# One layer of a streaming encoder in fp32: the order of loads around the output projection, the turn and the down sweep

## The chip, the cores and the metric

One core of a Trainium2 chip runs the whole layer. The metric is the device time of one execution in microseconds: the kernel before takes 1625.86 us, the median of three runs (1624.2 to 1626.41). The engines are TensorE (PE), VectorE (DVE), ScalarE (ACT), GpSimd (POOL) and SyncE (SP); all loads and most stores are issued from SP's queue, in its order.

## The reference

The layer has attention in two head groups, an output projection with a residual and a layer norm, a gated convolutional feed-forward block with a residual and a second norm, and a gated addition of a per-layer embedding. It runs for 1024 prompt rows and for 32 rows of a second request (the samples), with shared weights. What the change touches lies behind the attention, in `mix @ w_o` and the feed-forward block:

```python
mix = jnp.concatenate([o_a.reshape(b, s, H_A * D_VA), o_b.reshape(b, s, W_B)], -1)
return mix @ lp['w_o'], (c_kv, k_r, dk, dv)
...
u = h @ lp['w_up']                                  # 1024 -> 2 x 2816
up = jnp.concatenate([conv_state, u], 1)
z = lp['conv_b'] + sum(up[:, j:j + s] * lp['conv_w'][j] for j in range(CONV_W))
g, v = z[..., :D_FF], z[..., D_FF:]
out = (jax.nn.gelu(g, approximate=False) * v) @ lp['w_down']
...
h = _ln(ALPHA * x + a, lp['ln1_g'], lp['ln1_b'])
h = _ln(ALPHA * h + f, lp['ln2_g'], lp['ln2_b'])
gate = jax.nn.sigmoid(h @ lp['w_ple_gate'] + lp['b_ple_gate'])
y = h + gate * (p_emb @ lp['w_ple_proj'])
```

All inputs and outputs are fp32.

## The kernel before

**Arithmetic.** PE multiplies in fp32r, a rounded form of fp32. Each operand x is split into a high half (an ACT cast, L85) and a low half (a subtraction, L82, on DVE or POOL), and a product is three matmuls: high by high, high by low, low by high (`three`, L144 to L146). The 32 sample rows ride with high and low halves side by side and need two (`sample_rows`, L152 and L153). A weight tile is loaded to a staging tile by SP (`load`, L112) and split by ACT and DVE (`wload`).

**Tiles.** `pair()` takes a tile from a pool HP of 22 (names h...), `slab()` one of 4 (s...), `stg()` one of 2 staging tiles (t...); PSUM has four tiles pm and two pd. A tile's next user waits until its last reader is done. The rows are nine tiles of 128: 8 is the samples, and 7 down to 0 the prompt; `order` is 8, 7, ..., 0. The rows `arow(t)` hold x first, then h, then the output; four HP tiles hold the prompt's.

**The order of the work.** The program text is not the order on the engines. The kernel is built with a scheduler that simulates a timeline and places each instruction by it; dependencies, pool tiles and a `gate` (loads that may not go ahead of a named instruction) bind it. Each engine then runs its list strictly in that order.

**The stages.** Behind the attention, the mixed heads of a tile are split (`mix_in`), multiplied with w_o in four blocks of 256 columns (`wo_block`, `proj_rows`) and added to ALPHA times x (`residual`, L1026). Blocks 0 and 1 run over all tiles, block by block; blocks 2 and 3 run tile by tile in `h_rows`, which ends with the norm (`unit`) and a store of the normalised row to DRAM (`hrow`), since HP is needed for other things. `h_turn` transposes a row tile on PE (L1102) and copies it from PSUM with the norm's scale and bias applied (eight ACT activations, L1104). `h_pair` and `h_sample` make the operands of the up-projection from it, which is a Strassen-Winograd scheme: seven products (L1217 to L1219) on half-sized blocks, for each of two column halves b.

The up-projection runs over 22 pairs m of 128-wide blocks of the feed-forward width (`UpPair`). For each pair the weights are loaded two ahead (`up_load`), combined and split one ahead (`UpWeights.part`); `finish` gives six steps (`todo`: three taps of the convolution, gelu, gating, store to DRAM tensor `zd`), which run between the products of the next pair.

The down sweep runs over four groups of 6, 6, 6 and 4 blocks. For each group it takes the weights (`wdown`: a 512 KB load and a split per block) and then, per row tile, loads and splits z (`z_in`, 384 KB) and adds two 512-wide products to the row (`down_rows`); in group 0 the row is loaded back and multiplied with ln1 ahead of that (L1365, L1366). The last group is in `y_norm`, tile by tile together with the second norm, the gate and the output.

## Time and profile before

| | |
|---|---|
| median of three runs | 1625.86 us |
| profiled execution, its own time | 1623.54 us |
| its span | 1621.7 us |
| PE busy | 1515.6 us (93%) |
| DVE busy | 950.9 us (59%) |
| ACT busy | 724.2 us (45%) |
| POOL busy | 337.5 us (21%) |
| chain that ended last | PE 83%, DVE 7%, ACT 5%, DMA 3% |

The span is from the first to the last instruction of the profiled execution; its own time has some two microseconds around that. Busy time is an average over the whole layer; the stages named above lie one behind the other, the first w_o block from about 590 us, the turn about 706 to 738, the up-projection to about 1183, the down sweep's first three groups from 1202 to 1422, its last group to the end.

A row of the timeline gives start and duration of an instruction, engine, line, operation, output and input, and in brackets the idle time of its engine before it with what ended it.

### The profile page before, as it was taken

The page shows a single profiled execution, that of the slowest core. Times are in us where ns is not written, and L with a number is a line of the kernel's source. Part 1 is how long each engine was busy: PE and PEld are TensorE (multiplying, and loading weights), DVE is VectorE, ACT ScalarE, POOL GpSimd, SP SyncE. Part 2 cuts the span into 40 slices and gives each one's busy share as a digit, 9 for nine tenths or more (in the row PEclk, how much of TensorE's full clock was granted, in tenths as well). Part 3 has the DMA queues.
Part 4 walks back from the last instruction along what each step waited for, and adds up shares of the span by engine and source line. Part 5 has one row for each costly group of instructions (what it writes and reads, how often), then busy time and mean ns, then how long its engine had stood idle before and what let it go on. Part 6 is the DMA issues. An engine that isn't in the chain of part 4 may idle for free.

```text
span 1621.7 us, 25780 instructions
## 1 busy us (share of the span) xinstructions
PE 1515.6 (93%) x10015; PEld 1377.2 (85%) x10015; DVE 950.9 (59%) x1914; ACT 724.2 (45%) x1787; POOL 337.5 (21%) x394
## 2 busy tenths in 40 slices
PE   7999998888989979989999999999949999979998
PEld 7999987777878869979999999999938787856887
DVE  4013328786767655487677777777777524256332
ACT  4222438777777752185455555555442202111111
POOL 0002225532554310011011111111100000157311
PEclk9999999989999999999999999999979999989999
DMA  7112251311110241123122222222165424130111
GB/s 220 30 48 83 79 166 39 69 41 21 36 36 15 69 173 31 53 92 105 40 80 79 80 80 80 80 80 79 67 199 176 134 54 133 65 96 20 42 43 42
DMA packets 126943, 127.92 MB, mean 79 GB/s; under 512 B 14750, under 2 KB 107558, under 8 KB 126566
## 3 DMA queue, kind: packets, MB, share of 16 engines
q1 hardware_dynamic: 126821, 126.28, 25.6%
q8 instruction: 79, 1.29, 0.3%
q14 instruction: 43, 0.34, 0.1%
HBM read 93.83 MB, written 26.07 MB: 74 GB/s over the span
## 4 chain that ended last, share of the span: by engine, by line
PE 83%; DVE 7%; ACT 5%; DMA 3%; issue 1%; SPq 0%; POOL 0%; DVEq 0%; ACTq 0%
PE pm L144 14%; PE pm L146 14%; PE pm L145 14%; PE pd L1217 5%; PE pd L1219 5%; PE pd L1218 5%; PE pm L1217 4%; PE pm L1219 4%; PE pm L1218 4%; PE pm L813 2%; DVE h L82 2%; ACT h L85 2%; PE pm L152 1%; PE pm L153 1%; PE pm L579 1%
## 5 line engine op out<-in xcount | busy, mean ns | idle before, releaser
L144 PE MATMUL pm<-h,h 128*128 128x256 f32 (+4 forms) x1140 | 378.9, 332 | 13.3 <-ACT h L85 8.8
L146 PE MATMUL pm<-h,h 128*128 128x256 f32 (+4 forms) x1140 | 374.9, 330 | 2.6 <-DVE h L82 2.6
L145 PE MATMUL pm<-h,h 128*128 128x256 f32 (+4 forms) x1140 | 375.2, 329 | 0.0
L144 PEld LDWEIGHTS pm<-h,h 128*128 128x128 f32 x1140 | 217.7, 191 | 32.7 <-ACT h L85 9.6
L146 PEld LDWEIGHTS pm<-h,h 128*128 128x128 f32 x1140 | 216.2, 190 | 19.3 <-DVE h L82 3.0
L145 PEld LDWEIGHTS pm<-h,h 128*128 128x128 f32 x1140 | 216.7, 190 | 16.5 <-issue 0.5
L85 ACT CAST h<-t 128x1024 fp32r<-128x1024 f32 (+6 forms) x97 | 88.2, 920 | 232.6 <-PE pm L146 121.7
L82 DVE TENSOR_TENSOR h<-t,h 128x1024 fp32r<-128x1024 f32 (+6 forms) x87 | 92.4, 1071 | 106.7 <-ACT h L85 106.4
L82 DVE TENSOR_TENSOR h<-pm,h 128x256 fp32r<-128x256 f32 (+7 forms) x221 | 101.5, 485 | 55.8 <-ACT h L85 53.9
L1230 DVE SCALAR_TENSOR_TENSOR h<-h,cp,h 128x1058 f32<-128x1058 f32 x88 | 115.7, 1316 | 29.8 <-ACT h L1238 29.1
L1217 PE MATMUL pm<-h,s 128*128 128x264 f32 x360 | 103.1, 288 | 10.1 <-ACT s L85 10.1
L85 ACT CAST h<-pm 128x256 fp32r<-128x256 f32 (+7 forms) x221 | 88.2, 425 | 53.7 <-PE pm L804 22.2
L1204 ACT COPY h<-pd 128x256 f32<-128x256 f32 (+1 forms) x258 | 56.2, 270 | 118.0 <-PE pd L1219 117.7
L1218 PE MATMUL pm<-h,s 128*128 128x264 f32 x360 | 102.3, 286 | 0.0
L1219 PE MATMUL pm<-h,s 128*128 128x264 f32 x360 | 101.0, 288 | 0.2 <-DVE s L82 0.2
L1217 PE MATMUL pd<-h,s 128*128 128x264 f32 x344 | 98.1, 285 | 0.0
L1219 PE MATMUL pd<-h,s 128*128 128x264 f32 x344 | 98.0, 285 | 0.0
L1218 PE MATMUL pd<-h,s 128*128 128x264 f32 x344 | 97.9, 285 | 0.0
L82 DVE TENSOR_TENSOR h<-h,h 128x512 fp32r<-128x512 f32 (+3 forms) x160 | 93.1, 617 | 3.5 <-ACT h L85 2.1
L178 POOL TENSOR_TENSOR sm<-sm,neghalf 128x1 f32<-128x1 f32 (+1 forms) x37 | 24.2, 653 | 275.6 <-DVE sm L177 275.6
L1347 DVE TENSOR_TENSOR h<-pm,h 128x512 f32<-128x512 f32 x48 | 33.1, 689 | 82.3 <-PE pm L146 82.2
L1217 PEld LDWEIGHTS pm<-h,s 128*128 128x128 f32 x360 | 68.6, 191 | 10.7 <-ACT s L85 10.5
(319 smaller groups left out, 3728.3 us busy)
## 6 DMA issues: line engine op xcount, KB each, us to landing
h<-in_w_up SPq DMA_DIRECT2D x44, 512.0 KB, 4.5
zd<-h SPq DMA_DIRECT2D x22, 529.0 KB, 4.3
t<-in_w_down SPq DMA_DIRECT2D x22, 512.0 KB, 3.5
t<-zd SPq DMA_DIRECT2D x24, 384.0 KB, 4.0
h<-in_x_p SPq DMA_DIRECT2D x15, 512.0 KB, 6.9
t<-in_w_in SPq DMA_DIRECT2D x14, 512.0 KB, 4.0
h<-h SPq DMA_DIRECT2D x8, 512.0 KB, 4.3
t<-in_w_o SPq DMA_DIRECT2D x8, 512.0 KB, 3.6
```

The source lines that it names most:

```text
L82: return eng.tensor_tensor(out, x, y, ALU.subtract)
L85: c = ACT.copy(hi, src)
L144: PE.matmul(ps, sh, mh, start=(i == 0), stop=False)
L145: PE.matmul(ps, sh, ml, start=False, stop=False)
L146: PE.matmul(ps, sl, mh, start=False, stop=(i == last))
L813: PE.matmul(po[:, c : c + 256], vt[k // 4][:, k % 4, h % 4], pts[k // 4][:, hl, k % 4], start=(k == 0 and hl == 0), stop=(k == kt - 1 and ...
L1204: ACT.copy(x, y)
L1217: PE.matmul(ps[:, :BW], w[:, 0, k], c[:, k, 0], start=first and k == 0, stop=False, skip_group_check=True)
L1218: PE.matmul(ps[:, :BW], w[:, 0, k], c[:, k, 1], start=False, stop=False, skip_group_check=True)
L1219: PE.matmul(ps[:, :BW], w[:, 1, k], c[:, k, 0], start=False, stop=k == 3, skip_group_check=True)
L1230: DVE.scalar_tensor_tensor(z[:, j], U[:, j, i : i + T], cp[:, i, m + j * NF : m + j * NF + 1], z[:, j], ALU.mult, ALU.add)
L1347: DVE.tensor_tensor(d, ps[:n], d, ALU.add)
```

## The change

The loads and splits around these stages are issued at other places in the program; a few are also shaped differently.

1. **w_o stage.** Instead of all nine x rows at once, three are loaded first and the rest two tiles ahead inside the first loop, and the mixed heads are split two tiles ahead (before: one). The second w_o block is issued at the second tile. The last two 256-column blocks become one of 512, and `h_rows` has one 512-wide projection instead of two. The first up weights are loaded and combined in the second block's loop; before, they were combined between row tiles and products. The small convolution and norm tables are loaded ahead of the x rows, as the loops now stand behind them in the text.
2. **The turn.** `h_turn` copies odd blocks with DVE and even ones with ACT. The pair (1,1) and the samples' half 1 are made ahead of the last row tile, and all seven products of half 0 stand before the pair (1,0).
3. **Down sweep.** The six weights of group 0 are loaded as three tiles of two blocks (1 MB) during the last two up pairs and split between the products of the last pair. z, and in group 0 the rows, are fetched two tiles ahead; the next group's weights are issued at the fifth tile of each group; z of the first two tiles of the last group is fetched at the end of group 2. The last pair's finish steps run one per tile in group 0 instead of all before it. The rows' HP tiles are taken one by one, when the row comes back.

```diff
@@ -1045,28 +1045,13 @@
         (eng or POOL).tensor_tensor(r, r, g[:n, :D], ALU.mult)
         (eng or POOL).tensor_tensor(r, r, b[:n, :D], ALU.add)
-    for t in order:
+    def x_back(t):
         load(arow(t)[: TOK[t][1]], a["x_p"][t * 128 : (t + 1) * 128, :] if t < 8 else a["x_s"])
-    wb.append(wo_block(256, 256))
-    mix_in(order[1])
-    for i in range(2):
-        wb.append(wo_block(256 * (i + 2), 256))
-        for m, t in enumerate(order):
-            if i == 0 and 1 < m + 1 < 9:
-                mix_in(order[m + 1])
-            ps, ps2 = proj_rows(t, wo_at(wb[i], 256), 256)
-            residual(t, 256 * i, 256, ps, ps2)
-    hrow = [DR.tile([128, 1024], F32, name=nm("hrow")) for _ in range(8)]
-    def h_rows(t):
-        for i in (2, 3):
-            ps, ps2 = proj_rows(t, wo_at(wb[i], 256), 256)
-            residual(t, 256 * i, 256, ps, ps2)
-        unit(arow(t)[: TOK[t][1]], TOK[t][1])
-        if t < 8:
-            SP.dma_start(hrow[t], arow(t))
+    for t in order[:3]:
+        x_back(t)
+    for t in order[1:3]:
+        mix_in(t)
@@ -1101,7 +1086,10 @@
         for j in range(8):
             PE.transpose(ps[:, j, :n], arow(t)[:n, j * 128 : (j + 1) * 128], ident[:n, :n])
         for j in range(8):
-            ACT.activation(d[:, j], ps[:, j, :n], AF.Identity, bias=lnT[:, 8 + j : 9 + j], scale=lnT[:, j : j + 1])
+            if j % 2:
+                DVE.tensor_scalar(d[:, j], ps[:, j, :n], lnT[:, j : j + 1], lnT[:, 8 + j : 9 + j], ALU.mult, ALU.add)
+            else:
+                ACT.activation(d[:, j], ps[:, j, :n], AF.Identity, bias=lnT[:, 8 + j : 9 + j], scale=lnT[:, j : j + 1])
     def h_pair(b, q):
@@ -1258,9 +1246,37 @@
     zd = [DR.tile([128, len(fs), T], F32, name=nm("zd")) for fs in GROUPS]
+    for i in range(2):
+        for m, t in enumerate(order):
+            if i == 0:
+                if m == 1:
+                    wb.append(wo_block(256, 256))
+                if 2 < m + 2 < 9:
+                    x_back(order[m + 2])
+                    if m:
+                        mix_in(order[m + 2])
+            elif m == 0:
+                wb.append(wo_block(512, 512))
+                wts = UpWeights(up_load(0))
+            if i == 1 and m < NP:
+                wts.part(m)
+            ps, ps2 = proj_rows(t, wo_at(wb[i], 256), 256)
+            residual(t, 256 * i, 256, ps, ps2)
+    hrow = [DR.tile([128, 1024], F32, name=nm("hrow")) for _ in range(8)]
+    def h_rows(t):
+        ps, ps2 = proj_rows(t, wo_at(wb[2], 512), 512)
+        residual(t, 512, 512, ps, ps2)
+        unit(arow(t)[: TOK[t][1]], TOK[t][1])
+        if t < 8:
+            SP.dma_start(hrow[t], arow(t))
     for t in order[:4]:
         h_rows(t)
-    hs = slab()
+    hs = small(512, tag="sam", bufs=1)
     V["hs"], V["hs2"] = hs[:, :256].rearrange("p (k c) -> p k c", k=8), hs[:, 256:512]
     h_turn(8, V["hs"])
     h_rows(4)
@@ -1268,41 +1284,49 @@
     h_sample(0)
     h_rows(3)
     h_pair(0, 0)
-    R = up_load(0)
     h_rows(2)
-    wts = UpWeights(R)
-    wts.part(0)
-    wts.part(1)
     h_rows(1)
-    for i in range(2, 5):
-        wts.part(i)
+    h_pair(1, 1)
+    h_sample(1)
     h_rows(0)
     u = UpPair(0)
     u.ps[0, 0] = pm()
-    for i in range(3):
-        u.product(wts.w[i], i, 0)
-    h_pair(1, 1)
-    for i in range(3, 5):
-        u.product(wts.w[i], i, 0)
-    h_sample(1)
-    for i in range(5, NP):
-        wts.part(i)
+    for i in range(NP):
         u.product(wts.w[i], i, 0)
     h_pair(1, 0)
-    R = up_load(1)
-    nxt = UpWeights(R)
+    nxt = UpWeights(up_load(1))
+    gate[0] = None
+    acc = {}
+    wrows, wfirst = {}, []
+    def wd_load(fi):
+        wrows[fi // 2] = pair((128, 2, 1024), F32)
+        load(wrows[fi // 2], w_dn[:, fi : fi + 2])
+    def wd_part(fi):
+        w = pair()
+        split(w[:, 0, :1024], w[:, 1, :1024], wrows[fi // 2][:, fi % 2])
+        wfirst.append(w)
     todo = []
-    gate[0] = None
     for m in range(NF):
         if m:
             u = UpPair(m)
         if m + 2 < NF:
             R = up_load(m + 2)
+        else:
+            wd_load(2 * (m + 2 - NF))
         for i in range(NP):
             for b in range(2) if m else (1,):
                 u.product(wts.w[i], i, b)
             if m + 1 < NF:
                 nxt.part(i)
+            elif i < 6:
+                if i == 2:
+                    wd_load(4)
+                wd_part(i)
             if todo:
                 todo.pop(0)()
         todo = u.finish()
@@ -1311,11 +1335,7 @@
             nxt = UpWeights(R)
         if m == NF - 2:
             gate[0] = UnitF[0]
-    for s in todo:
-        s()
-    acc = [pair((128, 2, 1024), F32) for _ in range(4)]
     def wdown(fs, eng=None):
         return [wload([(0, 1024, w_dn[:, fi])], 1024, eng) for fi in fs]
@@ -1353,22 +1373,44 @@
     ln1 = [slab() for _ in range(2)]
     for i, key in enumerate(("ln1_g", "ln1_b")):
         load(ln1[i][:, :D], a[key].to_broadcast([128, D]))
+    def row_back(t):
+        n = TOK[t][1]
+        if t < 8 and t // 2 not in acc:
+            acc[t // 2] = pair((128, 2, 1024), F32)
+        r = arow(t)[:n]
+        if t < 8:
+            load(r, hrow[t])
+        DVE.tensor_tensor(r, r, ln1[0][:n, :D], ALU.mult)
+        DVE.tensor_tensor(r, r, ln1[1][:n, :D], ALU.add)
     gate_last = UnitF[0]
+    ahead = {}
+    def z_ahead(g, t):
+        if g == 0:
+            row_back(t)
+        ahead[g, t] = z_in(g, t)
+    ws = wfirst
+    for t in order[:2]:
+        z_ahead(0, t)
     for g in range(3):
-        ws = wdown(GROUPS[g])
-        for t in order:
+        for m, t in enumerate(order):
+            for c in (0, 512):
+                down_rows(g, t, ws, ahead[g, t], c)
+            if m + 2 < 9:
+                z_ahead(g, order[m + 2])
+            else:
+                z_ahead(g + 1, order[m - 7])
             if g == 0:
-                n = TOK[t][1]
-                r = arow(t)[:n]
-                if t < 8:
-                    load(r, hrow[t])
-                DVE.tensor_tensor(r, r, ln1[0][:n, :D], ALU.mult)
-                DVE.tensor_tensor(r, r, ln1[1][:n, :D], ALU.add)
-            z = z_in(g, t)
-            for c in (0, 512):
-                down_rows(g, t, ws, z, c)
-        if g == 0:
-            gate[0] = gate_last
+                for st in todo[:1]:
+                    todo.pop(0)()
+            if m == 4:
+                nxt = wdown(GROUPS[g + 1])
+        ws = nxt
+        gate[0] = gate_last
     ps = pm()
@@ -1381,7 +1423,6 @@
         SP.dma_start(d[j % 2].rearrange("(m p) -> m p", p=128), urow[:NM, j * 128 : (j + 1) * 128])
-    ws = wdown(GROUPS[3])
     w_gate = a["w_gate"].rearrange("(k p) c -> p k c", p=128)
     wg = [wload([(0, 1024, w_gate[:, k])], 1024, POOL if k % 2 else None) for k in range(8)]
     tabs = [pair((128, 2, T), F32) for _ in range(2)]
@@ -1402,7 +1443,7 @@
         split(d[:, :, 0, :n], d[:, :, 1, :n], ps[:, :2, :n])
     def y_norm(t):
-        z = z_in(3, t)
+        z = ahead.get((3, t)) or z_in(3, t)
         for c in (0, 512):
             down_rows(3, t, ws, z, c)
         norm(arow(t)[: TOK[t][1]], TOK[t][1], tabs[0][:, 0], tabs[0][:, 1])
```

What it moves, at three places. In the names, h, t, s and pm/pd are the pools' tiles, a number is a buffer, and `x2` means two of the kind in a row.

SP's queue around the w_o blocks (x_p are the prompt's rows, two per HP tile; acc_s takes the samples'). Before:

```order
L112 DMA t_6335<-in_w_o 128x4x256
L112 DMA acc_s<-in_x_s 32x1024
L112 DMA t_6340<-in_w_o 128x4x256
L112 DMA h_6315<-in_x_p 128x1024 x2
L112 DMA h_6314<-in_x_p 128x1024 x2
L112 DMA h_6313<-in_x_p 128x1024 x2
L112 DMA h_6312<-in_x_p 128x1024 x2
L112 DMA t_6354<-in_w_o 128x4x256
L112 DMA t_6359<-in_w_o 128x4x256
```

Now:

```order
L112 DMA acc_s<-in_x_s 32x1024
L1128 DMA t_6348<-in_ln_b 8x128
L112 DMA t_6392<-in_w_o 128x4x256
L112 DMA h_6315<-in_x_p 128x1024 x2
L112 DMA t_6397<-in_w_o 128x4x256
L112 DMA t_6670<-in_w_o 128x2x512
L112 DMA h_6314<-in_x_p 128x1024 x2
L112 DMA h_6313<-in_x_p 128x1024 x2
L112 DMA t_6675<-in_w_o 128x2x512
L112 DMA h_6312<-in_x_p 128x1024 x2
```

The second w_o block (t_6392 and t_6397; before, t_6335 and t_6340 were block 1 and t_6354 and t_6359 block 2) and part of the last one now stand among the rows.

DVE at the end of the up-projection, from its last reads of products (L1202 before, L1190 now) to the first row of the down sweep. The taps are L1230 before and L1218 now, L82 are low halves (128x1024 of a weight, 128x6x32 of the samples' z), L1365 and L1385 the row's multiplication with ln1. Before:

```order
L1202 TENSOR_TENSOR h_12959<-pd_12961,h_12959 128x8
L1241 TENSOR_TENSOR h_12958<-h_12958 128x1058
L1230 SCALAR_TENSOR_TENSOR h_13177<-h_12959,cp,h_13177 128x1058 x3
L82 TENSOR_TENSOR h_13203<-t_13201,h_13203 128x1024
L1230 SCALAR_TENSOR_TENSOR h_13177<-h_12959,cp,h_13177 128x1058
L82 TENSOR_TENSOR h_13208<-t_13206,h_13208 128x1024
L1241 TENSOR_TENSOR h_13177<-h_13177 128x1058
L82 TENSOR_TENSOR h_13213<-t_13211,h_13213 128x1024
L82 TENSOR_TENSOR h_13218<-t_13216,h_13218 128x1024
L82 TENSOR_TENSOR h_13223<-t_13221,h_13223 128x1024
L82 TENSOR_TENSOR h_13228<-t_13226,h_13228 128x1024
L82 TENSOR_TENSOR h_13233<-t_13234,h_13233 128x6x32
```

Now:

```order
L1190 TENSOR_TENSOR h_12732<-pd_12736,h_12732 128x8
L1218 SCALAR_TENSOR_TENSOR h_12731<-h_12486,cp,h_12731 128x1058
L82 TENSOR_TENSOR h_12806<-h_12488,h_12806 128x1024
L1218 SCALAR_TENSOR_TENSOR h_12731<-h_12486,cp,h_12731 128x1058
L82 TENSOR_TENSOR h_12840<-h_12734,h_12840 128x1024
L82 TENSOR_TENSOR h_12875<-h_12734,h_12875 128x1024
L82 TENSOR_TENSOR h_12907<-h_12838,h_12907 128x1024
L82 TENSOR_TENSOR h_12939<-h_12838,h_12939 128x1024
L82 TENSOR_TENSOR h_12979<-t_12980,h_12979 128x6x32
L1385 TENSOR_TENSOR h_12984<-h_12984,s_12973 128x1024
L1229 TENSOR_TENSOR h_12731<-h_12731 128x1058
```

Two of four taps, both gating products and one of the six low halves of weights no longer stand between the last product and the samples' z, and the weights come from HP tiles (h) instead of the staging ring (t).

SP's queue at the last group (zd_6926 before and zd_6370 now are its z; in_ln_g and in_ln_b the second norm's tables). Before:

```order
L112 DMA t_14590<-in_w_proj 128x1024
L112 DMA h_14585<-in_ln_g 128x1024
L112 DMA h_14585<-in_ln_b 128x1024
L112 DMA h_14586<-in_b_gate 128x1024
L112 DMA t_14595<-in_w_proj 128x1024
L1381 DMA out_conv_p<-sm_14519 44x128 x2
L1381 DMA out_conv_s<-sm_14519 44x128 x2
L112 DMA t_14601<-zd_6926 128x4x32
L112 DMA t_14643<-zd_6926 128x4x128
L112 DMA t_14687<-zd_6926 128x4x128
```

Now:

```order
L112 DMA t_14260<-zd_6370 128x4x32
L112 DMA t_14305<-zd_6370 128x4x128
L112 DMA t_14320<-in_w_gate 128x1024
...
L112 DMA t_14365<-in_w_proj 128x1024
L1423 DMA out_conv_p<-sm_14314 44x128 x2
L1423 DMA out_conv_s<-sm_14314 44x128 x2
L112 DMA h_14360<-in_ln_g 128x1024
L112 DMA h_14360<-in_ln_b 128x1024
L112 DMA h_14361<-in_b_gate 128x1024
L112 DMA t_14370<-in_w_proj 128x1024
L112 DMA t_14452<-zd_6370 128x4x128
```

z of tiles 8 and 7 moved ahead of the eight w_gate loads; z of tile 6 stands where that of tile 8 stood, behind the second w_proj load.

## The prediction

> **What bounds the kernel now.** I read the busy time of each engine in stretches of the span first, then PE's instructions with what ended the idle time before them, then what the engine or queue named there did. Seven rows of the table by stretches (columns: PE, PEld, DVE, ACT and POOL busy us with counts, the granted TensorE clock, DMA share, GB/s):
>
> ```profile
> 590.00:616.00 26.00, 14.76 (x100) 13.90 (x100) 13.89 (x30) 16.26 (x46) 0.00 (x0) 0.80 0.72 262
> 706.00:738.00 32.00, 21.52 (x146) 20.22 (x145) 27.43 (x57) 24.70 (x69) 2.60 (x4) 0.84 0.36 116
> 740.00:1160.00 420.00, 420.00 (x3451) 420.00 (x3450) 317.59 (x580) 220.62 (x573) 63.45 (x101) 1.00 0.23 73
> 1174.00:1208.00 34.00, 12.21 (x62) 8.76 (x62) 23.06 (x23) 14.71 (x20) 2.88 (x5) 0.70 0.50 166
> 1220.00:1420.00 200.00, 200.00 (x865) 160.02 (x865) 87.25 (x104) 43.57 (x49) 7.98 (x4) 1.00 0.37 110
> 1420.00:1438.00 18.00, 9.71 (x34) 5.95 (x33) 6.11 (x8) 4.79 (x7) 6.27 (x3) 0.72 0.53 167
> 1440.00:1600.00 160.00, 160.00 (x735) 125.75 (x735) 74.14 (x113) 25.58 (x39) 65.91 (x42) 1.00 0.12 38
> ```
>
> PE sets the time: it is busy 420 of 420 us in the up-projection and 200 of 200 and 160 of 160 in the down sweep. Nothing the change does to other engines inside those stretches is worth anything, as long as they keep up. What can be gained from rescheduling lies in four places where PE runs dry: A (590 to 616, the first w_o block), B (706 to 738, the turn into the up-projection), C (1174 to 1208, up- to down-projection) and D (1420 to 1438, into the last group). The idle times there are 26 − 14.76 = 11.2, 32 − 21.52 = 10.5, 34 − 12.21 = 21.8 and 18 − 9.71 = 8.3 us.
>
> After each gap PE also runs slowly for a while. PE alone in stretches of 5 us (busy, count, clock, DMA share, GB/s), right behind two gaps and later with the same shapes:
>
> ```profile
> 608.00:613.00 5.00, 4.54 (x19) 0.50 0.70 207
> 620.00:625.00 5.00, 5.00 (x44) 1.00 0.00 0
> 1202.00:1207.00 5.00, 4.81 (x12) 0.50 0.88 271
> 1240.00:1245.00 5.00, 5.00 (x23) 1.00 0.36 122
> ```
>
> Behind the gap at 608 there are 25 matmuls too few at 5.00/44 = 0.114 us, 2.8 us; behind that at 1202 eleven too few at 0.217, 2.4 us. So a closed gap returns its idle time and about 2.5 us more, and a gap that only shrinks may keep the 2.5. All four are worth at most 11.2 + 10.5 + 21.8 + 8.3 + 4 × 2.5 = 61.8 us. The Trainium skill, "TensorE: Matmul & The Clock Gate" (Part 1: The HAM clock gate), says that about 3.4 us without work halves the clock and that about 3.4 us of sustained work restores it. The clock of 0.50 behind these gaps agrees; by that rule any remainder above 3.4 us pays the restart in full, which is a result of its own among the rivals.
>
> **A: x rows and w_o.** PE (first two rows), ACT, SP's queue, and three rows of the page's DMA issues (their last number is the time to landing):
>
> ```profile
> 597.62 0.38 PE L146 MATMUL pm<-h,h 128*128 128x256 f32 x1 [2.37 <-DVE h L82]
> 608.03 0.58 PE L144 MATMUL pm<-h,h 128*128 128x256 f32 x1 [7.54 <-ACT h L85]
> ...
> 605.40 1.04 ACT L85 CAST h<-t 128x1024 fp32r<-128x1024 f32 x1 [8.84 <-DMA t<-in_w_o]
> ...
> 590.16 4.14 SPq L112 DMA_DIRECT2D h<-in_x_p x8
> 596.12 13.21 SPq L112 DMA_DIRECT2D t<-in_w_o x4
> ...
> t<-zd SPq DMA_DIRECT2D x24, 384.0 KB, 4.0
> ...
> h<-in_x_p SPq DMA_DIRECT2D x15, 512.0 KB, 6.9
> ...
> t<-in_w_o SPq DMA_DIRECT2D x8, 512.0 KB, 3.6
> ```
>
> Eight x rows of 512 KB stand ahead of the w_o loads, so the cast of a w_o half waits 8.84 us for its DMA and the matmuls behind it in PE's order wait 7.54. The order of SP now puts only two x rows ahead of the second w_o block's second half. Tile 7 needs that first x pair and no later w_o block; the next tile can start where the first now ends. I count the 2.37, the 7.54 and the 2.8 us of slow clock, 12.7, and let a microsecond go at tile 5, whose products are interleaved with the next tile's in the new order: 12 us. Bounds: 14.0 (11.2 + 2.8, nothing left) and 8, if at tile 5 a w_o load is met uncovered for its whole 3.6 us and slows the clock (14.0 − 3.6 − 2.4).
>
> **The merged w_o block.** PE in 20 us with 256-wide and with 512-wide products:
>
> ```profile
> 620.00:640.00 20.00, 20.00 (x171) 1.00 0.03 8
> 1240.00:1260.00 20.00, 20.00 (x88) 1.00 0.45 121
> ```
>
> Each row tile had two blocks of 24 matmuls at 20/171 = 0.117 us and gets one of 24 at 20/88 = 0.227: 5.61 − 5.45 = 0.16 us a tile, 1.4 us over nine (the samples' 32 become 16). It is on PE's path in full stretches, so it counts: 1.4.
>
> **B: the turn.** PE, then ACT, then three groups of the whole span (count, busy us, mean ns):
>
> ```profile
> 717.51 0.39 PE L1217 MATMUL pm<-h,s 128*128 128x264 f32 x1 [2.62 <-ACT s L85]
> 732.23 0.59 PE L1217 MATMUL pm<-h,s 128*128 128x264 f32 x1 [7.43 <-ACT s L85]
> ...
> 725.89 5.78 ACT L1104 ACTIVATE h<-pd,lnT 128x128 f32<-128x128 f32 x16
> 731.37 0.80 ACT L85 CAST s<-h 128x512 fp32r<-128x512 f32 x1
> ...
> L1104 ACT ACTIVATE h<-pd,lnT 128x128 f32<-128x128 f32 x64 | 23.1, 541 | 6.4 <-PE pd L1102 6.4
> L82 DVE TENSOR_TENSOR h<-pm,h 128x128 fp32r<-128x128 f32 x48 | 13.2, 284 | 6.0 <-ACT h L85 5.4
> ```
>
> Sixteen copies out of PSUM take ACT 5.78 us, and the cast that PE waits for stands behind them. Eight of each sixteen go to DVE. DVE has no such row; its nearest is the 128x128 read of PSUM at 284 ns, so eight cost about 2.3 us there, and ACT's eight 5.78/2 = 2.9: the copies end about 3 us earlier. The pair (1,1) also moves ahead of the last row tile, so its casts no longer stand between the first products and the last pair. Against this: DVE is busy 27.43 of the 32 us already, 32 copies (32 × 0.28 = 9 us) are added to it over the stage, and the first product's PSUM is read by ACT only behind the casts of pair (1,1) in the new order. By counts from that order times these rows DVE has some 64 us of work where PE has 66, so the two are level and each late piece shows on PE. I take half of 10.5 + 2.5 = 13.0: 6.5 us. Bounds 0 (DVE simply replaces ACT) and 13.
>
> **C: into the down sweep.** PE, SP's queue, ACT, DVE, then two groups:
>
> ```profile
> 1182.51 0.28 PE L1219 MATMUL pd<-h,h 128*128 128x264 f32 x1
> 1202.19 0.66 PE L152 MATMUL pm<-h,h 128*64 128x512 f32 x1 [19.40 <-DVE h L82]
> ...
> 1187.09 2.70 SPq L112 DMA_DIRECT2D t<-in_w_down x2
> 1192.63 2.85 SPq L112 DMA_DIRECT2D t<-in_w_down x2
> ...
> 1196.14 1.04 ACT L85 CAST h<-t 128x1024 fp32r<-128x1024 f32 x1 [2.28 <-DMA t<-in_w_down]
> ...
> 1180.67 2.67 DVE L1230 SCALAR_TENSOR_TENSOR h<-h,cp,h 128x1058 f32<-128x1058 f32 x2
> 1199.71 1.23 DVE L82 TENSOR_TENSOR h<-t,h 128x1024 fp32r<-128x1024 f32 x1 [1.27 <-ACT h L85]
> ...
> L1230 DVE SCALAR_TENSOR_TENSOR h<-h,cp,h 128x1058 f32<-128x1058 f32 x88 | 115.7, 1316 | 29.8 <-ACT h L1238 29.1
> L82 DVE TENSOR_TENSOR h<-t,h 128x1024 fp32r<-128x1024 f32 x48 | 58.3, 1224 | 80.7 <-ACT h L85 80.5
> ```
>
> The last up product ends about 1182.8; the six weights pass two at a time through a ring of two staging tiles, and PE waits 19.40 us. In the new order the three 1 MB loads are issued under the last two pairs, so the loads leave the path. What remains is DVE's: behind the last read of a product stand, before the sample's z (the first thing PE needs), two taps, five low halves and the low half of z. At 1.316 and 1.224 us, some 0.1 us less each back to back, that is 2 × 1.23 + 5 × 1.15 + 0.3 = 8.5 us. DVE begins such a run about 2.1 us before PE's end (1180.67 in the row), so PE waits 8.5 − 2.1 = 6.4 us and still restarts slowly. Gain 19.40 − 6.4 = 13.0, and 1 more for the 2.4 us of short stalls before it (21.8 − 19.4), half of which I let go: 14. Bounds: 24.2 (21.8 + 2.4) if DVE has done the splits earlier, and 10 if the row and z loads, which queue behind the last z write, make the second tile wait some 4 us. The writes to zd, the six finish steps and ln1 are only moved: they cost DVE the same, under PE's full sweep, where DVE was busy 87 of 200 us.
>
> **D: into the last group.** PE, SP's queue, and the group of POOL's splits (every other w_gate tile, and w_proj):
>
> ```profile
> 1430.25 0.69 PE L152 MATMUL pm<-h,h 128*64 128x512 f32 x1 [8.29 <-DVE h L82]
> ...
> 1421.66 0.33 SPq L112 DMA_DIRECT2D t<-in_w_proj  x1
> 1424.27 10.99 SPq L112 DMA_DIRECT2D t<-zd  x4
> ...
> L82 POOL TENSOR_TENSOR h<-t,h 128x1024 fp32r<-128x1024 f32 x8 | 19.8, 2475 | 233.4 <-ACT h L85 233.4
> ```
>
> PE stopped at 1430.25 − 8.29 = 1421.96; z of tile 8 was issued 2.3 us later, behind w_proj, and was ready 8.3 later. Now z of tiles 8 and 7 comes first: 16 + 24 matmuls at 0.227 cover 9.1 us. Then comes z of tile 6, in the very queue place where tile 8's stood. At the old pace it is ready at 8.3 plus about 0.6 for a wider split, just in time. But two staging buffers and two pairs are now held by z, so two of the eight w_gate tiles are split later, and the load passes w_proj with them. Two POOL splits more behind the group's end, 2 × 2.475 us, put z some 5 us later (14 instead of 9). I take a stall of 4 and a restart of 2 against 8.3 + 2.5: gain 4. Bounds: 10.8 (old pace) and −2 (stall of 10, restart kept).
>
> **Sum.** 12 + 1.4 + 6.5 + 14 + 4 = 37.9 us. The profiled execution took 1623.54 us (span 1621.7), so 1585.6; it lay 2.3 under the median of the runs, 1625.86, so **1588 us**.
>
> **Rivals.** First, all four gaps close to less than the idle time that slows the clock: 61.8 + 1.4 less some 6 of short stalls, about 57: 1569 us. For it: all that PE waited for are DMAs or casts that now stand earlier; against it: DVE's list at C. 10%. (By the clock-gate rule cited above the difference to my forecast is then two restarts, 5 us, and the idle time.)
>
> Second, the gaps only move, since the staging ring and the tile pool let the earlier loads go no sooner: the lower bounds together, 8 + 1.4 + 0 + 10 − 2 = 17: 1608 us. For it: in C the loads already waited for the two staging tiles, not for the program. 15%.
>
> Third, slower: the next group's six w_down loads now stand in SP's queue ahead of the last two tiles' z (and rows, in the first group). From 1187.09 to 1192.63 two of them took 5.54 us, so six take 16.6; with z's landing (4.0 in the row under A) and a split of a low half (1.2 at most), z comes some 22 us later, while PE has three tiles of 36 matmuls, 24.5 us. The margin is about 2 us. If the pool has no tile free for the next weights until the old are done, each of three changes of group costs what C cost, 19.4 + 2.4: 65 us, less 38: 1653 us. It decides from 13 us a change on, where the gain is gone. Against it: before, the same loads crossed the same changes with PE at 200 of 200. 4%.
>
> That nothing reaches PE (the scheduler rebuilds the old order) has 1%: the new order differs at all four places.
>
> **Numbers.** The forecast has 70%, its own range 1577 to 1600. With most of the second rival and part of the first, 8 in 10 lie in 1573 to 1606. A difference of 0.2% (3 us) is about what can be told from none. Faster takes the forecast and two rivals, 0.95; same 0.01; slower 0.04.
>
> **What would show it.** In the new profile: no PE wait above 2 us near 600; in the turn, DVE named as the releaser instead of ACT's cast; at the end of the up-projection one gap of about 6 us released by DVE's low halves, with clock 0.5 behind it; into the last group no wait at tile 8 and one of about 4 us two tiles later, released through z. 512-wide products at 0.227 in the second half of w_o. I am wrong if C's gap is still above 10 us or gone, or if PE waits at a change of group inside the sweep.

## The result, and the profile after

The changed kernel takes 1589.27 us, the median of four runs (1588.82 to 1590.73), against 1625.84 us before: a ratio of 0.9778, 95% interval 0.9761 to 0.9795, so 2.2% or 36.6 us faster. Forecast were 1588 us and a range of 1573 to 1606. The profiled execution took 1588.82 us with a span of 1586.7, 35.0 less than the span before.

The busy time of the engines after, by stretches (columns as in the prediction):

```profile
590.00:616.00 26.00, 25.10 (x208) 24.54 (x208) 20.63 (x50) 16.79 (x48) 0.00 (x0) 1.00 0.70 258
694.00:732.00 38.00, 30.78 (x204) 28.68 (x203) 35.31 (x81) 24.79 (x69) 1.94 (x6) 0.87 0.32 94
740.00:1140.00 400.00, 400.00 (x3280) 400.00 (x3279) 302.22 (x547) 211.58 (x551) 59.10 (x96) 1.00 0.25 77
1160.00:1174.00 14.00, 8.39 (x44) 5.94 (x43) 13.20 (x15) 9.01 (x14) 2.90 (x4) 0.88 0.52 171
1200.00:1380.00 180.00, 180.00 (x777) 143.38 (x776) 77.48 (x94) 38.30 (x45) 4.82 (x2) 1.00 0.37 110
1388.00:1408.00 20.00, 13.74 (x55) 9.47 (x54) 15.18 (x18) 5.29 (x7) 10.81 (x6) 0.84 0.50 176
1420.00:1580.00 160.00, 160.00 (x739) 125.90 (x738) 64.37 (x97) 25.38 (x39) 55.21 (x36) 1.00 0.11 36
```

PE is still full in the long stretches, and so are the changes of group inside the sweep. In place A it no longer runs dry at all (25.10 of 26; the 0.9 left was there before). B, C and D are still there, smaller. Their longest waits, in PE's timeline after:

```profile
706.29 3.67 PE L1087 MATMUL pd<-ident,h 128*128 128x128 f32 x16 [3.79 <-DVE h L1090]
710.87 0.59 PE L1205 MATMUL pm<-h,s 128*128 128x264 f32 x1 [0.90 <-ACT h L1192]
1169.84 0.66 PE L152 MATMUL pm<-h,h 128*64 128x512 f32 x1 [3.82 <-DVE h L82]
1403.42 0.79 PE L144 MATMUL pm<-h,h 128*128 128x512 f32 x1 [5.24 <-ACT h L85]
1406.52 0.80 PE L146 MATMUL pm<-h,h 128*128 128x512 f32 x1 [1.02 <-DVE h L82]
```

Where the 35 us lie follows from marks that both timelines have in common. At 590 us the two timelines agree within 0.02 us.

| stretch of PE's timeline | before | after | gained | forecast |
|---|---|---|---|---|
| 590.0 to the first up product (A, and the merged block) | 120.0 | 106.2 | 13.8 | 12 + 1.4 |
| first to 1000th up matmul (B) | 140.4 | 138.3 | 2.1 | 6.5 |
| 1000th up matmul to the end of the last | 332.3 | 331.6 | 0.8 | 1 (short stalls of C) |
| last up product to the first of the sweep (C) | 19.4 | 3.8 | 15.6 | 13 |
| first to 600th of the sweep (with the slow restart) | 141.2 | 140.6 | 0.6 | 0 |
| 600th of the sweep to the last matmul (D) | 273.6 | 271.9 | 1.7 | 4 |

The last column adds up to 37.9 with the merged block, the gains, before rounding, to 34.7 of the 35.0. The sum came so near because errors of opposite sign met: B and D gave less, C gave more. That is luck. The experiments below are about these, and about what in A did the work.

Two things move a single profile without any edit near them. Before 590 us nothing is changed, yet the matmul that stands at 590 us here comes up to 2.7 us later in other variants' profiled executions; lengths are therefore counted from that matmul (the common mark) or from a stage's own start. And the half clock that comes with a wait of some microseconds lasts 3.4, 6.8 or 10.2 us, in steps of 3.41 us, and not always the same number of steps for the same wait. PE alone in the turn, in the changed kernel, in a variant with the same turn (group 0's weights late, under C) and in one with a shorter wait (two of eight copies on DVE, under B):

```profile
702.00:722.00 20.00, 13.92 (x80) 0.74 0.49 132
702.00:722.00 20.00, 13.09 (x90) 0.91 0.47 132
702.00:722.00 20.00, 15.39 (x107) 0.91 0.56 159
```

The granted clock of 0.74 stands for 10 of these 20 us at half clock, 0.91 for some 3.5.

### The profile page after: what moved, and what is told of

The parts are those of the page before. It is cut to its first block, busy times and chain, and to the rows that moved or that the text cites. A ratio compares the mean times of both kernels' runs of the same rounds, so it can differ in the third digit from the quotient of the medians.

```text
span 1586.7 us, 25344 instructions
## 1 busy us (share of the span) xinstructions
PE 1514.8 (95%) x9807; PEld 1367.4 (86%) x9807; DVE 962.0 (61%) x1940; ACT 714.2 (45%) x1750; POOL 334.2 (21%) x394
## 4 chain that ended last, share of the span: by engine, by line
PE 84%; DVE 8%; ACT 4%; issue 2%; DMA 1%; POOL 1%; SPq 0%; DVEq 0%; ACTq 0%; POOLq 0%
PE pm L146 14%; PE pm L144 14%; PE pm L145 14%; PE pd L1207 5%; PE pd L1206 5%; PE pd L1205 5%; PE pm L1205 4%; PE pm L1207 4%; PE pm L1206 4%; DVE h L82 3%; PE pm L813 2%; ACT h L85 2%; PE pm L579 1%; PE pm L804 1%; DVE h L562 1%
## 5 line engine op out<-in xcount | busy, mean ns | idle before, releaser
L144 PE MATMUL pm<-h,h 128*128 128x512 f32 (+4 forms) x1076 | 367.8, 342 | 9.5 <-ACT h L85 6.1
L146 PE MATMUL pm<-h,h 128*128 128x512 f32 (+4 forms) x1076 | 364.2, 339 | 1.3 <-DVE h L82 1.3
L145 PE MATMUL pm<-h,h 128*128 128x512 f32 (+4 forms) x1076 | 364.0, 339 | 0.0
L144 PEld LDWEIGHTS pm<-h,h 128*128 128x128 f32 x1076 | 205.0, 191 | 31.7 <-ACT h L85 6.8
L146 PEld LDWEIGHTS pm<-h,h 128*128 128x128 f32 x1076 | 203.6, 189 | 21.5 <-DVE h L82 2.2
L145 PEld LDWEIGHTS pm<-h,h 128*128 128x128 f32 x1076 | 204.1, 190 | 19.5 <-issue 0.5
L85 ACT CAST h<-t 128x1024 fp32r<-128x1024 f32 (+6 forms) x91 | 82.1, 911 | 215.4 <-PE pm L146 103.6
L82 DVE TENSOR_TENSOR h<-t,h 128x1024 fp32r<-128x1024 f32 (+6 forms) x81 | 88.5, 1101 | 99.2 <-ACT h L85 99.1
L82 DVE TENSOR_TENSOR h<-pm,h 128x256 fp32r<-128x256 f32 (+7 forms) x221 | 101.6, 485 | 54.9 <-ACT h L85 52.9
L1218 DVE SCALAR_TENSOR_TENSOR h<-h,cp,h 128x1058 f32<-128x1058 f32 x88 | 115.7, 1315 | 25.5 <-ACT h L1226 24.8
L82 DVE TENSOR_TENSOR h<-h,h 128x512 fp32r<-128x512 f32 (+4 forms) x166 | 100.7, 638 | 2.2 <-ACT h L85 2.1
L82 DVE TENSOR_TENSOR s<-h,s 128x512 fp32r<-128x512 f32 (+1 forms) x96 | 60.3, 638 | 28.6 <-ACT s L85 28.3
L1190 DVE TENSOR_TENSOR h<-pm,h 128x256 f32<-128x256 f32 (+1 forms) x178 | 43.6, 286 | 52.7 <-ACT h L1192 37.1
```

The source lines that it names most:

```text
L82: return eng.tensor_tensor(out, x, y, ALU.subtract)
L85: c = ACT.copy(hi, src)
L144: PE.matmul(ps, sh, mh, start=(i == 0), stop=False)
L145: PE.matmul(ps, sh, ml, start=False, stop=False)
L146: PE.matmul(ps, sl, mh, start=False, stop=(i == last))
L1190: UnitF[0] = DVE.tensor_tensor(x, y, x, ALU.add)
```

## The experiments

Each kernel is the changed one with the edit shown. Medians are of four runs.

### A: x rows or mixed heads?

With all x rows loaded at once again, the heads still split two tiles ahead:

```diff
-    for t in order[:3]:
+    for t in order:
         x_back(t)
...
-                if 2 < m + 2 < 9:
-                    x_back(order[m + 2])
```

> The changed kernel with all x rows loaded at once again, so that the second half of the second w_o block stands behind all eight prompt rows in SP's queue; the mixed heads stay two tiles ahead. Theory 1, the place of the x rows and that of the heads count together: ACT's cast of that half waits for its DMA until about 605 us as before and holds the heads of tile 5 behind it, while PE's tiles 7 and 6 last until about 601.5: PE waits 4 to 5 us once and its clock falls, time 1594 to 1597. Rival, the heads split two ahead are enough alone: PE waits 1 us or less, time 1588 to 1590.

With the heads one tile ahead, the x rows still two ahead:

```diff
-    for t in order[1:3]:
+    for t in order[1:2]:
         mix_in(t)
...
-                    if m:
-                        mix_in(order[m + 2])
+                if 1 < m + 1 < 9:
+                    mix_in(order[m + 1])
```

> The changed kernel with the mixed heads split one tile ahead, as before; the x rows stay two tiles ahead. Theory 1 (both count together): tile 6's heads stand behind ACT's cast of a w_o half again, but that half lands at 598.3 us instead of 605, so PE waits 1 to 3 us near 600 and the time is 1590 to 1592.5. Rival, the order on ACT alone makes the wait: 5 us or more, time 1595 to 1600.

The first took 1597.10 us (1594.9 to 1598.34), 7.8 more. Its PE and ACT:

```profile
607.84 0.58 PE L144 MATMUL pm<-h,h 128*128 128x256 f32 x1 [5.80 <-ACT h L85]
...
606.43 1.04 ACT L85 CAST h<-t 128x1024 fp32r<-128x1024 f32 x1 [7.46 <-DMA t<-in_w_o]
607.38 7.46 ACT L85 CAST h<-h 128x256 fp32r<-128x256 f32 x24
```

From the common mark the first up product comes 9.0 us later. The chain can be read here: ACT waits 7.46 us for a w_o half that lands late behind eight x rows; the casts of the heads (24 of 128x256) stand behind it on ACT; PE, which has no use for that w_o half yet, waits for the heads. The second took 1589.62 us (1587.75 to 1590.07), no difference from 1589.27; PE waited 0.77 and 0.73 us. In its profile the first up product still comes 2.0 us later from the common mark, and the turn behind it is 2.5 us shorter (135.8 instead of 138.3), with waits as long but 3.4 instead of 10.2 us at half clock. So of the two parts that theory 1 named, the order of the loads is the large one, and the heads' place is worth about 2 us at most. With the w_o half landing at 597 or 598 us instead of 606, the heads behind its cast come almost in time even one tile ahead.

### B: what bounds the turn

All copies on ACT; two of eight on DVE; and the pair (1,1) put back to its old place:

```diff
-            if j % 2:
+            if False:          # all on ACT
+            if j % 4 == 3:     # two of eight on DVE
```

```diff
-    h_pair(1, 1)
-    h_sample(1)
     h_rows(0)
...
     for i in range(3):
         u.product(wts.w[i], i, 0)
+    h_pair(1, 1)
...
+    h_sample(1)
```

> The changed kernel with all eight copies of each transposed row tile on ACT again, everything else as changed. In the changed kernel's profile PE waits 3.79 us at 702.5 for a DVE copy and DVE is busy 35.3 of the 38 us from 694. Theory 1, DVE is the bound of the turn: 32 copies of about 0.36 us leave DVE (11 us), the 3.79 us wait goes or halves, and the time is 1585 to 1588. Rival, the copies on ACT were the bound and the split is what made the turn shorter: waits released by ACT come back, the 2 us that the turn gained are lost, and the time is 1591 to 1594.

> The changed kernel with two of eight copies on DVE and six on ACT. Theory 1 (DVE is the bound of the turn, ACT has 13 us to spare of the 38): 16 copies of 0.36 us move, the wait of 3.79 us becomes 1 or less, time 1585 to 1587. Rival (ACT is the bound or becomes it): 1589 to 1592, with PE's waits in the turn released by ACT.

> The changed kernel with the pair (1,1) and the samples' half 1 put back behind three of the first seven products, as before the change; copies stay split between ACT and DVE. If moving this pair ahead was what shortened the turn: the first products of the second half wait 5 us or more again and the time is 1592 to 1596. Rival, the order of the pair is worth nothing since DVE's sum of work sets the turn: 1588 to 1590. Third, the move put DVE work ahead of the last row tile and cost the 3.79 us wait: 1585 to 1587.

| kernel | median us (range) | first to 1000th up matmul, us |
|---|---|---|
| before (8 on ACT, old order) | 1625.84 | 140.4 |
| changed (4 on ACT, 4 on DVE) | 1589.27 (1588.82 to 1590.73) | 138.3 |
| all 8 on ACT | 1591.66 (1589.67 to 1593.88) | 137.5 |
| 6 on ACT, 2 on DVE | 1583.07 (1582.89 to 1584.86) | 132.9 |
| 4 and 4, pair in its old place | 1590.02 (1588.68 to 1592.31) | 136.9 |

The last column needs a scale. Five variants that leave the turn as in the changed kernel (all x rows at once, both kernels under C, both under D) took 136.3 to 138.5 us for it, with PE's waits at 7.0 to 8.1 us in sum and 3.4 to 10.2 us at half clock. A difference of less than 2 us in this column shows nothing about an edit.

One row of the table by stretches for each: 4 and 4 with the old place, all on ACT (a narrower window, where it is tightest), and two on DVE:

```profile
694.00:732.00 38.00, 28.74 (x203) 27.10 (x203) 36.82 (x84) 24.96 (x66) 2.36 (x5) 0.91 0.34 102
```

```profile
700.00:726.00 26.00, 18.36 (x118) 17.27 (x117) 18.12 (x40) 23.66 (x70) 1.50 (x2) 0.80 0.41 122
```

```profile
694.00:732.00 38.00, 33.39 (x245) 31.72 (x244) 34.34 (x77) 26.32 (x74) 2.64 (x7) 0.96 0.43 125
```

With four on DVE, DVE is busy 35.31 of 38 us (36.82 in the kernel with the old place, where PE waits 8.90 us in one piece, released by a DVE copy). With none, ACT is busy 23.66 of 26 and PE's waits are released by ACT (3.69 us of them by its reads of the first products). Two on DVE leaves both some air and shortens the turn by 5.4 us, by 3.4 against the shortest of those five; PE's waits there fell from 7.2 to 4.6 us, the rest is half clock (0.91 against 0.74 in the rows above). The whole kernel is 6.2 us faster, more than its forecast of 1585 to 1587, though the wait did not go to 1 us: one of 3.27, released by ACT, took its place. So "DVE is the bound" was right for the changed kernel, and "ACT becomes the bound" for the one without the split: the turn is a balance, and the half-and-half split only moved the bound. That is why all on ACT gained nothing that can be told in the turn (137.5 us). Its time missed the forecast of 1585 to 1588, but not by the turn: in its profile the last group, from the sweep's 600th matmul, took 274.9 us instead of 271.9, told at the end. Where the pair (1,1) stands is worth nothing that can be told (1590.02 against 1589.27; its last group took 274.3).

### The merged block of w_o

```diff
-                wb.append(wo_block(512, 512))
+                wb.append(wo_block(512, 256))
+                wb.append(wo_block(768, 256))
```

with two projections per tile in `h_rows` as before the change.

> The changed kernel with the last 512 columns of the output projection as two blocks of 256 again. If PE's matmul time counts in full there (0.117 us for 256 wide against 0.227 for 512 wide, 8 x 48 against 8 x 24 of them, and the samples): 1.4 us slower, 1590 to 1591.5, and the first product of the up-projection starts 1.4 us later. Rival, DVE sets this stage's end, so that PE's saving is given back in the waits behind it: 1589 to 1589.5, with the first product later and the waits smaller by as much.

It took 1590.24 us (1590.04 to 1590.75). The 0.97 us to 1589.27 looks like the forecast 1.4, but it does not lie there: measured from PE's common mark at 590 the 1000th up matmul comes after 242.6 us with two blocks and after 244.5 with one. The first up product is 2.7 us later with two blocks, and the stage behind it 4.6 shorter (133.7 against 138.3). Neither figure is the block's. Sixteen transposes (1.9 us of PE) stand ahead of the first up product with two blocks and behind it with one, and the turn had 3.4 us at half clock instead of 10.2. The like case is the kernel with group 0's weights late (under C), which is the changed one up to there and also had 3.4 us: 242.5 us from the mark with one block, 0.8 us more of it waits, against 242.6 with two. So next to nothing of what one block saves PE is left at that point, as the rival said. The 0.97 us in the time lie behind this stage and are not explained.

### C: the gap into the sweep

Group 0's weights at the start of the sweep as before, with the last pair's finish steps ahead of them; and two of their low halves on POOL:

```diff
-        else:
-            wd_load(2 * (m + 2 - NF))
...
-            elif i < 6:
-                if i == 2:
-                    wd_load(4)
-                wd_part(i)
...
-    ws = wfirst
+    for s in todo:
+        s()
+    todo = []
+    ws = wdown(GROUPS[0])
```

```diff
-        split(w[:, 0, :1024], w[:, 1, :1024], wrows[fi // 2][:, fi % 2])
+        split(w[:, 0, :1024], w[:, 1, :1024], wrows[fi // 2][:, fi % 2], POOL if fi in (2, 4) else None)
```

> The changed kernel, but group 0's six weights are loaded and split at the start of the sweep as before, and the last pair's finish steps run ahead of it; all else as changed. Theory: these loads through the two staging tiles were the 19.40 us wait, and their move under the last pairs is what took it to 3.82: it comes back to 17 to 20 us, released by DVE's low half behind DMAs of w_down, and the time is 1603 to 1607. Rival, z and rows fetched two tiles ahead did most of it: the wait is 8 us or less and the time is 1589 to 1595.

> The changed kernel with two of the six low halves of group 0's weights subtracted on POOL. Theory, DVE's list behind the last product is all that is left of the gap into the sweep (3.82 us): it is 2 x 1.15 us shorter, PE waits 1.5 us or less, the clock does not fall, time 1585.5 to 1588. Rival, POOL and DVE slow each other while both subtract (in the changed kernel a DVE low half took 2.58 instead of 1.23 us while POOL ran one of 2.40): DVE's remaining ones stretch, POOL's end at 2.4 us each behind their casts, the wait is 3.8 or more, time 1589 to 1591.

The first took 1607.71 us (1605.9 to 1609.74), 18.4 more, and PE waits as before:

```profile
1185.09 0.66 PE L152 MATMUL pm<-h,h 128*64 128x512 f32 x1 [19.92 <-DVE h L82]
```

In this wait ACT's casts of the last four weights waited for their DMA each time, 0.88 to 2.59 us, so it is the loads that count and not the finish steps. About half of the whole gain is these six weights; z and rows fetched ahead do not replace them.

The second took 1592.52 us (1590.66 to 1594.44): slower by 3.2, though DVE has two instructions less. PE, then DVE and POOL of this kernel:

```profile
1170.41 0.66 PE L152 MATMUL pm<-h,h 128*64 128x512 f32 x1 [5.82 <-DVE h L82]
...
1162.13 3.44 DVE L1218 SCALAR_TENSOR_TENSOR h<-h,cp,h 128x1058 f32<-128x1058 f32 x1
1165.49 4.50 DVE L82 TENSOR_TENSOR h<-h,h 128x1024 fp32r<-128x1024 f32 x2
...
1161.61 2.85 POOL L82 TENSOR_TENSOR h<-h,h 128x1024 fp32r<-128x1024 f32 x1 [0.48 <-ACT h L85]
1165.58 3.33 POOL L82 TENSOR_TENSOR h<-h,h 128x1024 fp32r<-128x1024 f32 x1
```

A tap took 3.44 instead of 1.31 us: it ended at 1165.57, 1.1 us after POOL's instruction (1164.46), about its own length. The two low halves took 4.50 instead of 2.3 and ended 1.1 us after POOL's second, which itself took 3.33 us where POOL's low halves take 2.4 elsewhere: it began beside the first of DVE's two. The rival was right in kind, and the price was higher than its 1589 to 1591: DVE does not run such an instruction beside POOL's, it waits for it, and POOL for DVE. The Trainium skill, "GPSIMD Engine Reference" (1. Specifications), says that POOL's SBUF interfaces are shared with DVE and that DVE instructions with two SBUF inputs contend; taps and low halves have two, and this trace agrees. These durations show how much: the one stands still for what is left of the other's instruction.

### D: into the last group

z of a third tile ahead of w_gate; and no split on POOL:

```diff
                 z_ahead(g + 1, order[m - 7])
+                if g == 2 and m == 8:
+                    z_ahead(3, order[2])
```

```diff
-    wg = [wload(..., 1024, POOL if k % 2 else None) for k in range(8)]
+    wg = [wload(..., 1024) for k in range(8)]
...
-    wp = [wload(..., 1024, POOL) for k in range(2)]
+    wp = [wload(..., 1024) for k in range(2)]
```

> The changed kernel with z of a third tile (6) of the last group fetched ahead of the w_gate loads. Theory, the 5.24 us wait in the last group is tile 6's z behind w_gate and w_proj in the queue: PE does one tile more (24 matmuls, 5.5 us) before it needs the next z, the wait of 5.24 and that of 1.02 behind it go to 1 or less and the time is 1582 to 1585. Rival, z of tile 6 takes one more tile of the pool, so w_gate is split later still and the wait only moves to tile 5 or to the gate: 1588 to 1590.

> The changed kernel with all splits of w_gate and w_proj on DVE, none on POOL. Theory, POOL's splits (2.4 to 2.6 us each, and DVE is slowed while they run: 2.58, 2.39 and 2.13 us where it takes 1.23 and 0.68) hold the staging tiles and so z of tile 6: the wait of 5.24 us shrinks to 1 to 3, time 1585.5 to 1588. Rival, the loads themselves and the free tiles of the pool set it: 1588.5 to 1590.

| kernel | median us (range) | PE's waits in D, us | 600th matmul of the sweep to the last, us |
|---|---|---|---|
| before | 1625.84 | 8.29 | 273.6 |
| changed | 1589.27 (1588.82 to 1590.73) | 5.24 and 1.02 | 271.9 |
| third z ahead | 1588.07 (1586.52 to 1588.43) | 1.85 and 1.44 | 267.1 |
| no split on POOL | 1586.77 (1585.88 to 1587.73) | 3.99 and 0.67 | 269.5 |

The stage's length answers for the first: it is 4.7 us shorter with one more z, since PE had a tile more to do. Its waits are 3.0 us less, and it had 3.4 us at half clock instead of 10.2. The profiled execution was only 2.2 us shorter in all, as the part ahead of the change, which no edit touches, was 2.3 us longer in it (its first up product came at 698.5 instead of 696.2); the medians differ by 1.2, which is in the rival's range. The waits did not go to 1 or less; they sit at the next tile, whose z is behind w_gate and w_proj in its turn. Without POOL z of tile 6 was issued at 1397.82, 2.0 us before PE ran dry, instead of 1.2 us after it (1399.35), so the staging tiles did come free sooner. The wait shrank by 1.25 us only, to 3.99 where 1 to 3 was expected: ACT took z behind w_proj, whose data it waited for until 1402.17. The time of 1586.77 was in the forecast.

### Together

```diff
two of eight copies on DVE, z of a third tile ahead, no split on POOL (best_two);
the same with one of eight copies on DVE (best_one)
```

> The changed kernel with three edits together: two of eight turn copies on DVE and six on ACT, z of a third tile of the last group fetched ahead of w_gate, and all splits of w_gate and w_proj on DVE. If the gains add, they are 6.2 (1589.27 less 1583.07) and 4.7 for the last group (its time from the sweep's 600th matmul in the third run), the gate's 2.3 overlapping in part: 1576 to 1579. Rival, the last group's splits on DVE and the earlier z stand in each other's way: 1580 to 1583.

> As best_two, but with one of eight turn copies on DVE and seven on ACT. If DVE still bounds the turn (it was busy 34.3 of 38 us with two of eight, ACT 26.3): 8 copies of 0.36 us less, 0.5 to 2 us faster than best_two. Rival, what is left is ACT's (a wait of 3.27 us there was released by ACT's read of the first products behind its casts): the same or up to 2 us slower than best_two.

The first took 1580.81 us (1579.88 to 1581.61), a ratio of 0.9728 to before (0.9714 to 0.9743) and 8.5 us less than the changed kernel: the fastest of all here. It missed its 1576 to 1579 and fell in the rival's range, since the gains in the last group do not add (269.4 us from the sweep's 600th matmul, where the third z alone gave 267.1). PE waits there again, a tile later; its z was issued at 1397.90, just after DVE's low half of w_proj (1395.25, 2.62 us) had ended:

```profile
1401.75 0.50 PE L144 MATMUL pm<-h,h 128*128 128x512 f32 x1 [4.19 <-ACT h L85]
```

The second took 1583.60 us (1582.34 to 1585.1), 2.8 more: with seven copies a wait of 3.77 us in the turn is released by ACT, and the rival was right in direction. But of the 4.1 us between the two profiles only 1.1 lie in the turn (133.9 against 132.9) and 3.2 between the 1000th up matmul and the sweep's 600th, where half clock with an equal wait (3.72 and 3.71 us) lasted 10.2 instead of 3.4 us.

## Why the prediction was right, and where it was not

**A was right in size, loose in its mechanism.** Forecast 12, measured 13.8 with the merged block. With two blocks it is about 11.1 to the first up product (698.9 instead of 710.05, counted from the common mark), with the 1.9 us of the sixteen transposes that stand ahead of it there, so 13.0. The prediction said that PE's matmuls waited behind a cast of w_o. What stood behind that cast were the heads of the next tile, on ACT; the w_o half itself was not needed yet. The kernel with all x rows at once shows it. The x rows' place in SP's queue is what counts. The stall expected at tile 5 did not come: SP, then ACT after the change:

```profile
593.62 4.39 SPq L112 DMA_DIRECT2D t<-in_w_o  x2
598.05 2.17 SPq L112 DMA_DIRECT2D h<-in_x_p  x4
...
598.32 1.05 ACT L85 CAST h<-t 128x1024 fp32r<-128x1024 f32 x1 [1.46 <-DMA t<-in_w_o]
599.27 7.48 ACT L85 CAST h<-h 128x256 fp32r<-128x256 f32 x24
```

**The merged block failed as a term.** 1.4 us were counted "on PE's path in full stretches". The stretch was full, but behind it lay waits for DVE and ACT: at the 1000th up matmul 0.1 us of it was left between like cases.

**B is the step that was mis-sized most.** Forecast 6.5, half of 13.0, measured 2.1: PE's waits fell from 10.5 to 7.2 us, and the half clock stayed at 10.2 us. In the five variants with the same turn the place gave 1.9 to 4.1; with two of eight copies on DVE it gave 7.5 (140.4 less 132.9). The prediction had DVE's list level with PE's (64 and 66 us) and the bound 0 "DVE simply replaces ACT", which is nearly what happened; choosing the middle between the bounds was the error, as the count already said that there was no air. A copy on DVE also cost more than the 284 ns of the nearest row. DVE after the change:

```profile
700.83 0.39 DVE L1090 TENSOR_SCALAR h<-pd,lnT 128x128 f32<-128x128 f32 x1
702.66 0.80 DVE L1090 TENSOR_SCALAR h<-pd,lnT 128x128 f32<-128x128 f32 x2
```

**C was right in kind and too small.** DVE's list behind the last product is what the prediction counted, in the same order, and as long: from 1161.21 to 1169.69, 8.5 us.

```profile
1161.21 1.31 DVE L1218 SCALAR_TENSOR_TENSOR h<-h,cp,h 128x1058 f32<-128x1058 f32 x1
1162.44 1.22 DVE L82 TENSOR_TENSOR h<-h,h 128x1024 fp32r<-128x1024 f32 x1
1163.58 1.31 DVE L1218 SCALAR_TENSOR_TENSOR h<-h,cp,h 128x1058 f32<-128x1058 f32 x1
1164.81 4.62 DVE L82 TENSOR_TENSOR h<-h,h 128x1024 fp32r<-128x1024 f32 x4
1169.35 0.34 DVE L82 TENSOR_TENSOR h<-t,h 128x192 fp32r<-128x192 f32 x1
```

What was mis-sized is its head start. The prediction took 2.1 us from the profile before; DVE began 4.8 us ahead of PE's end (1166.03), so PE waited 3.82 instead of 6.4. The restart was shorter as well, but by chance. PE in the 5 us behind C's gap in the changed kernel, and in the one with all x rows at once:

```profile
1169.84:1174.84 5.00, 5.00 (x16) 0.71 0.77 261
1178.25:1183.25 5.00, 5.00 (x12) 0.50 0.76 257
```

The gap is 3.82 us in the one and 3.81 in the other, with the same work behind it. With 23 matmuls at full speed, 7 are lost at 0.217 us (1.5 us) in the first and 11 in the second, as before the change. Six profiled executions have this gap: four kept 15 or 16 matmuls at a clock of 0.66 to 0.71, two kept 12 at 0.50 (the other is the kernel with two blocks of w_o). By the clock-gate rule that the prediction cited from the Trainium skill, a remainder over 3.4 us pays the restart in full, and a shorter one none. The traces bear out neither half as stated, and the measurement decides: 3.8 us cost part of it or all, and half clock also came with waits of 2.62 us (before, ending at 717.51), 3.00 (two blocks, 707.77) and 3.27 (two copies on DVE, 708.95). The Trainium skill, "TensorE: Matmul & The Clock Gate" (Part 1: The HAM clock gate), adds that the window runs freely, so that the number of slow matmuls varies from run to run; the six executions agree.

**D was right in kind.** Tiles 8 and 7 went through without a wait and the next z was late, as forecast; 5.24 us instead of 4, and a second wait of 1.02. The half clock behind it lasted 10.2 us, as before, so nothing of the restart was gained; measured 1.7. The prediction's own terms, a stall of 4 and a restart of 2 against 8.3 + 2.5, leave 4.8 and not the 4 that it took. SP, ACT and DVE after:

```profile
1396.57 0.33 SPq L112 DMA_DIRECT2D t<-in_w_proj  x1
1399.35 7.66 SPq L112 DMA_DIRECT2D t<-zd  x2
...
1401.27 1.04 ACT L85 CAST h<-t 128x1024 fp32r<-128x1024 f32 x1 [5.17 <-DMA t<-in_w_proj]
...
1404.36 2.10 DVE L82 TENSOR_TENSOR h<-t,h 128x512 fp32r<-128x512 f32 x1
```

z of tile 6 was issued at 1399.35, behind w_proj, and its low half then took 2.10 us instead of 0.69, beside POOL. That second price was not in the prediction.

**The rivals.** That the changes of group would stall was wrong (180 of 180 us busy). That the gaps only move was right for D and, through DVE, for B. No gap but A closed.

## What to carry to other kernels

Where an engine runs its list strictly in order, ask of each instruction that waits for a DMA what stands behind it; in A a weight that nobody needed yet held the operands that PE was waiting for, and the cure was the order of the loads. When work is moved to relieve one engine, count both lists: half-and-half gave 2 to 4 of 13 us, two of eight gave 7.5. A term on a full stretch of the bounding engine counts only if nothing else sets the end of that stretch. And before a microsecond or two in a stage is put down to an edit, see how long the half clock lasted in both profiles: here it moved the same turn by 2 us.

## What the runs showed of the hardware

The half clock that came with a wait of PE lasted a multiple of 3.41 us in every profile here from 590 us on, and nearly equal waits got different multiples: 3.79 to 3.87 us in the turn came with 3.4 (group 0's weights late), 6.8 (all x rows at once) or 10.2 us (the changed kernel).

A DVE instruction with two SBUF inputs does not share time with a POOL tensor instruction on SBUF tiles, it waits for it, even for two in a row. In the kernel with all copies on ACT, a low half of 128x512 (0.69 us alone) met two POOL instructions back to back in the last group; DVE, POOL and PE there:

```profile
1405.45 4.32 DVE L82 TENSOR_TENSOR h<-t,h 128x512 fp32r<-128x512 f32 x1
...
1404.57 2.35 POOL L1045 TENSOR_TENSOR acc_s<-acc_s,h 32x1024 f32<-32x1024 f32 x1 [0.92 <-DVE acc_s L1040]
1406.88 2.33 POOL L82 TENSOR_TENSOR h<-t,h 128x1024 fp32r<-128x1024 f32 x1
...
1409.82 0.79 PE L146 MATMUL pm<-h,h 128*128 128x512 f32 x1 [3.57 <-DVE h L82]
```

It took 4.32 us and ended 0.56 us after POOL's second. In the changed kernel the same low half went ahead of POOL's second and took 2.10. In both it began 0.88 us after POOL's first, so the start does not decide it, and the trace does not show what does. Of nine profiles in which the three meet in this way, DVE went first in seven; POOL did in the kernels with all copies on ACT and with the pair in its old place, whose edits lie 700 us earlier. PE then waits 3.57 or 3.52 us at this point instead of 1.02 in the changed kernel.

An input from PSUM instead makes the difference. DVE, then POOL of the changed kernel:

```profile
1413.80 0.69 DVE L1367 TENSOR_TENSOR h<-pm,h 128x512 f32<-128x512 f32 x1
1414.45 1.03 DVE L82 TENSOR_TENSOR h<-t,h 128x512 fp32r<-128x512 f32 x1
...
1412.52 2.42 POOL L1045 TENSOR_TENSOR h<-h,h 128x1024 f32<-128x1024 f32 x1 [1.36 <-DVE h L1040]
```

The first reads one input from PSUM and kept its 0.69 us beside POOL; the second reads both from SBUF and ended 0.54 us after it.
